# One hybrid encoder layer: which stages run beside which, and a 512-wide out-projection

## The chip, the cores and the metric

The kernel runs on one core of a Trainium2 chip. The core has five engines with instruction queues of their own: TensorE (PE in the profile; its weight loads are listed as PEld), VectorE (DVE), ScalarE (ACT), GpSimd (POOL) and SyncE (SP), which here issues every DMA. SBUF is the working memory, PSUM holds matmul results in eight banks, DRAM holds inputs, outputs and scratch tensors. The metric is device microseconds (us) of one execution.

## The reference

One layer, for a prompt of 1024 tokens and for 8 decode streams of 16 new tokens each, which share the weights. The kernel packs both into 9 tiles of 128 tokens (8 of the prompt, one of all samples). All is float32; D_MODEL 1024, 16 heads of 64, half of them in group A and half in B.

```python
h = rmsnorm(x, g_mix)
q_a, k_a, v_a, q_b, k_b, v_b = split_heads(h, w_in)      # w_in: 1024 x 3072
# group A, causal, full past: stick-breaking
z = q_a @ k_a * 64 ** -0.5
w = exp(log_sigmoid(z) + sum of log_sigmoid(-z) over the keys behind, strictly causal)
a = w @ v_a
# group B, own chunk of 64 and the 8 chunks before: softmax with a relative bias
o_b = softmax(q_b @ k_b * 64 ** -0.5 + bias) @ v_b
x = x + concat(rmsnorm(a, g_out_sb), rmsnorm(o_b, g_out_cb)) @ w_out
h = rmsnorm(x, g_ffn)
x = x + (silu(h @ w_gate) * (h @ w_up)) @ w_down         # width 2816
x = x + sigmoid(rmsnorm(x, g_ple) @ w_ple_gate) * (p @ w_ple_proj)
y = rmsnorm(x, g_final)
```

The prompt attends to itself. Each decode stream attends to its cache (A: 1024 past keys, B: 512) and its own 16 tokens. The new keys and values are outputs too.

## The kernel before

**Arithmetic.** Every matrix product is three matmuls (`mm3`, L103 to L106) of a high and a low part of each operand: high x high, high x low, low x high. So each operand is split: ScalarE copies the high part, GpSimd (weights, V caches) or VectorE (what comes out of PSUM) subtracts it for the low part (`Chunks.parts`, L148 and L109).

**Stages.** The source lists them in this order, some as generators that yield after each step, so that `advance(main, side, ratio)` can take steps of two in turn:

1. Norm of the 9 token tiles and their transposes into `hT` (L187 to L197).
2. `qkv_group(0)`: A's projection, k, v, then q, 256 columns of `w_in` at a time. k and v are made token tile by token tile (24 matmuls of 256 columns, then a yield; 18 yields for two chunks); q comes out transposed, three token tiles at a time (24 matmuls of 384 columns, 12 yields). Results go to the DRAM tensors `qkT` and `vhl`, in parts.
3. `qkv_group(1)`, B's projection, beside `decode` at 0.8 decode steps per projection step. `decode` runs through A's 8 streams and then B's; a step handles 256 cached keys (512 KB, tile `draw`): a K chunk is transposed (L367), split (`dhi`, `dlo`) and multiplied with q (`sdec`); a V chunk is split and multiplied with the transposed weights (L442, L443). A stream has 4 K and 4 V chunks in A, 2 and 2 in B. `RAWS` = 2 chunks are held raw. A's weights come from a sigmoid on ScalarE (L400), the causal factor and 1 - w on GpSimd (L412, L414) and a running product on VectorE (L416).
4. `attention(range(8))`: 8 pairs of heads (4 of A, 4 of B), 128 units of one head and 128 queries, over the prompt. A unit's scores come from L555 and L556. In A two sigmoids give `w` and `keep` (L560, L561), VectorE scans `keep` (L569), GpSimd multiplies (L570); in B VectorE adds the bias `toep` and takes the maximum (L564), ScalarE takes the exponential (L573). Five units later (`LAG`) the weights are transposed (L589), split (`wth`, `wtl`) and multiplied with v (L612, L613). `finish` normalises a pair of heads and writes it to the DRAM tensor `mixp` (L631 to L654). In the first 64 steps `embed` (p @ w_ple_proj, tile `pj`, stored in `proj`) runs beside it at 0.5 and decode at 0.4, in the next 48 decode at 0.7, then what is left of decode.
5. The last 25 steps of attention beside `half_out` at 1.5: `mix` reads `mixp` back, transposes and scales it into `hU` (L816 to L825), 12 steps for the four pairs of A; then A's half of the out-projection in 4 column chunks of 256, 36 steps of 12 matmuls.
6. `mix` for B's four pairs, one step of `half_out` beside each of its 12, the rest of `half_out`, then `lower`: B's half of the out-projection with the FFN norm and its transposes.
7. FFN, per-layer embedding gate, final norm.

**What sets the order.** The source gives dependencies and a priority; the tile framework then lays out one fixed order of instructions for each engine at build time. An instruction can come ahead of its place in the source when its operands are ready. Each engine works through its own order. Tiles of one tag share `bufs` buffers, and a tile waits for the release of the buffer that it takes; pools on the left and right side of SBUF and of the PSUM banks (`banks`) are opened and closed like stacks, so a new stage's tile waits for the old tiles in its place. `ch` is the weight pool: one raw buffer (`wraw`) and two pairs of `whi`, `wlo`. The attention borrows these: `qk` and `vk` take the tags `whi` and `wlo`, `osb` in `finish` takes `wraw`.

## Time and profile before

| | |
|---|---|
| median of 3 runs | 1923.48 us (1921.3 to 1924.91) |
| profiled execution | 1920.99 us, span of the trace 1919.2 us |
| PE matmuls | busy 1833.9 us (96% of the span), 11998 instructions |
| VectorE | busy 823.2 us (43%) |
| ScalarE | busy 718.2 us (37%) |
| GpSimd | busy 722.3 us (38%) |
| DMA | 220.60 MB, mean 115 GB/s |
| granted PE clock | 0.991 of full speed |

The span is the time from the first to the last instruction on the core; the run time has about 1.8 us around it. Busy time is the union of an engine's instructions. Matmuls overlap each other in the pipeline, so that a row's duration is longer than the distance to the next one's start. In rows of groups, the columns are: line, engine, operation, tiles (out<-in), shapes, count | busy us, mean ns of one | idle time of the engine just before them, and what ended it. All steps of one kind share the line of their helper: L104 to L106 are every `mm3`, L109 every low part, L133 every load of weights and caches.

### The profile page before, as it was taken

What the parts mean: (1) busy time and instruction counts of PE and PEld (TensorE: products, weight loads), DVE (VectorE), ACT (ScalarE), POOL (GpSimd) and SP (SyncE); (2) the same over time, 40 slices, a digit from 0 to 9 for tenths busy, and PEclk for the clock granted to TensorE, in tenths of its full rate; (3) what the DMA queues carried; (4) which work ended last, traced back from release to release, by engine and by line L of the source; (5) the groups of instructions that cost most, each with busy time, mean ns of one, the idle gap of its engine ahead of it and who ended that gap; (6) DMA issues with size and microseconds to landing.
All of it is one profiled execution on the core that took longest, in us unless ns stands there. A gap on an engine that the chain in (4) does not pass through costs nothing.

```text
span 1919.2 us, 30012 instructions
## 1 busy us (share of the span) xinstructions
PE 1833.9 (96%) x11998; PEld 1733.7 (90%) x11998; DVE 823.2 (43%) x1590; ACT 718.2 (37%) x1545; POOL 722.3 (38%) x600
## 2 busy tenths in 40 slices
PE   7999999988888798899999999999999999999998
PEld 7999999987777688889999999999999999999898
DVE  5201332347888888783541331321322312313735
ACT  5322444347778687872241111111111111121532
POOL 4232345446567744523022223223223223122355
PEclk9999999999999899999999999999999999999999
DMA  6555556576558576773011111111111101111133
GB/s 214 201 176 177 183 192 203 172 229 184 161 144 218 150 223 196 214 234 117 12 45 45 44 44 44 44 45 44 45 44 44 44 29 38 44 45 44 36 98 132
DMA packets 166011, 220.60 MB, mean 115 GB/s; under 512 B 14576, under 2 KB 118768, under 8 KB 165872
## 3 DMA queue, kind: packets, MB, share of 16 engines
q1 hardware_dynamic: 165872, 218.69, 37.2%
q8 instruction: 95, 1.56, 0.4%
q14 instruction: 44, 0.36, 0.1%
HBM read 168.84 MB, written 49.81 MB: 114 GB/s over the span
## 4 chain that ended last, share of the span: by engine, by line
PE 61%; DVE 5%; DMA 3%; ACT 3%; POOL 2%; issue 1%; SPq 0%; POOLq 0%; ACTq 0%; DVEq 0%
PE ps L104 16%; PE ps L105 16%; PE ps L106 16%; PE acc L104 2%; PE acc L106 2%; DVE keep L569 2%; PE acc L105 2%; DMA draw<-in_cache_cb_v 1%; PE pt L589 1%; DVE wtl L109 1%; PE pt L613 1%; PE pt L187 1%; PE pt L612 1%; PE pt L367 1%; ACT dhi L148 1%
## 5 line engine op out<-in xcount | busy, mean ns | idle before, releaser
L109 POOL TENSOR_TENSOR wlo<-wraw,whi 128x1024 fp32r<-128x1024 f32 (+1 forms) x118 | 257.2, 2200 | 605.1 <-ACT whi L148 605.1
L106 PE MATMUL ps<-hUh,wlo 128*128 128x384 f32 x1056 | 352.9, 334 | 0.0
L104 PE MATMUL ps<-hUh,whi 128*128 128x384 f32 x1056 | 352.9, 334 | 0.0
L105 PE MATMUL ps<-hUl,whi 128*128 128x384 f32 x1056 | 352.9, 334 | 0.0
L148 ACT CAST whi<-wraw 128x1024 fp32r<-128x1024 f32 (+1 forms) x118 | 107.6, 962 | 328.0 <-PE ps L106 227.4
L923 DVE TENSOR_TENSOR x<-x,ps 128x512 f32<-128x512 f32 x198 | 135.9, 687 | 158.3 <-PE ps L106 158.3
L104 PEld LDWEIGHTS ps<-hUh,whi 128*128 128x128 f32 x1056 | 198.2, 188 | 0.4
L105 PEld LDWEIGHTS ps<-hUl,whi 128*128 128x128 f32 x1056 | 198.2, 188 | 0.4
L106 PEld LDWEIGHTS ps<-hUh,wlo 128*128 128x128 f32 x1056 | 198.2, 188 | 0.0
L104 PE MATMUL ps<-whi,hTh 128*128 128x256 f32 x576 | 165.4, 287 | 0.7 <-ACT sth L215 0.6
L105 PE MATMUL ps<-wlo,hTh 128*128 128x256 f32 x576 | 164.6, 286 | 1.0 <-POOL wlo L109 1.0
L106 PE MATMUL ps<-whi,hTl 128*128 128x256 f32 x576 | 165.0, 287 | 0.0
L109 POOL TENSOR_TENSOR dlo<-draw,dhi 128x1024 fp32r<-128x1024 f32 x48 | 117.8, 2455 | 102.1 <-ACT dhi L148 95.3
L105 PE MATMUL ps<-wlo,acth 128*128 128x512 f32 x396 | 156.2, 394 | 0.0
L104 PE MATMUL ps<-whi,acth 128*128 128x512 f32 x396 | 155.3, 392 | 0.0
L106 PE MATMUL ps<-whi,actl 128*128 128x512 f32 x396 | 153.8, 388 | 0.0
L909 DVE TENSOR_TENSOR tmp<-sg,ps 128x384 f32<-128x384 f32 x66 | 36.6, 555 | 235.4 <-PE ps L106 235.4
L907 DVE TENSOR_TENSOR sg<-tmp,ps 128x384 f32<-128x384 f32 x66 | 36.5, 554 | 197.7 <-ACT tmp L906 197.7
L109 POOL TENSOR_TENSOR actl<-tmp,acth 128x384 fp32r<-128x384 f32 x66 | 66.5, 1007 | 133.8 <-ACT acth L910 133.8
L105 PEld LDWEIGHTS ps<-wlo,hTh 128*128 128x128 f32 x576 | 111.0, 193 | 1.3 <-POOL wlo L109 1.3
L104 PEld LDWEIGHTS ps<-whi,hTh 128*128 128x128 f32 x576 | 111.0, 193 | 1.1 <-ACT sth L215 0.8
L569 DVE TENSOR_TENSOR_SCAN keep<-keep,zero 128x128 f32<-128x128 f32 (+3 forms) x64 | 105.7, 1658 | 14.1 <-ACT keep L561 11.0
(187 smaller groups left out, 4439.4 us busy)
## 6 DMA issues: line engine op xcount, KB each, us to landing
draw<-in_cache_sb_k SPq DMA_DIRECT2D x32, 512.0 KB, 4.4
draw<-in_cache_sb_v SPq DMA_DIRECT2D x32, 512.0 KB, 3.9
wraw<-in_w_in SPq DMA_DIRECT2D x12, 1024.0 KB, 5.5
wraw<-in_w_gate SPq DMA_DIRECT2D x11, 1024.0 KB, 5.4
wraw<-in_w_up SPq DMA_DIRECT2D x11, 1024.0 KB, 5.5
wraw<-in_w_down SPq DMA_DIRECT2D x11, 1024.0 KB, 4.9
v<-sv SPq DMA_DIRECT2D x12, 768.0 KB, 4.1
x<-in_x_prompt SPq DMA_DIRECT2D x16, 512.0 KB, 6.4
```

The costliest lines, as they stand in the source:

```text
L104: T.matmul(out, lhsT=ah, rhs=bh, start=start, stop=False)
L105: T.matmul(out, lhsT=ah, rhs=bl, start=False, stop=False)
L106: T.matmul(out, lhsT=al, rhs=bh, start=False, stop=stop)
L109: eng.tensor_tensor(out, a, hi.bitcast(F32), op=ALU.subtract)
L148: A.copy(h[:, o], v[:, o])
L187: T.transpose(pt[:, j * P : (j + 1) * P], h[:, c : c + P], ident)
L367: T.transpose(pt[:, pr * P : (pr + 1) * P], raw[:, m, pr * P : (pr + 1) * P], ident)
L569: V.tensor_tensor_scan(rev, rev, zero[:, 0:1].to_broadcast([P, n]), 1.0, op0=ALU.mult, op1=ALU.add)
L589: T.transpose(pt[:, (c - c0) * P : (c - c0 + 1) * P], w[:, c * P : (c + 1) * P], ident)
L907: V.tensor_tensor(out[0][:, f, s], t_, ps, op=ALU.mult)
L909: V.tensor_tensor(t_, sg[:, f, s], ps, op=ALU.mult)
L923: V.tensor_tensor(x1[t][:, o], x1[t][:, o], ps, op=ALU.add)
```

## The change

Stages are paired in another way.

- `qkv` replaces the two calls of `qkv_group`: A's q, A's k, of A's v the third token group (tiles 6 to 8, in which the samples are) of both column chunks, 36 steps that run alone; then the rest of A's v and B's k, 30 steps; then B's v and B's q, 30 steps.
- `decode` takes its group as an argument and is made twice. Decode A runs beside the 30 steps of A's v and B's k at 2.2. Decode B runs beside B's attention, followed by `embed` (`chain`), at 1.3 for 42 attention steps.
- The attention's first 58 steps run beside B's v and q (1.95 per projection step), 42 beside decode B and `embed`, the last 37 beside `half_out` at 1.0.
- In decode, `keep` is a second sigmoid on ScalarE; the causal mask is a matmul that adds -1e30; V chunks come `VLAG` items later; `RAWS` is 4.
- `qk` and `vk` have buffers of their own; `keep` in the attention has three buffers for four, `obt` one for two, `stl` one for two.
- v is split and written per token tile (36 writes of one tile for 12 of three).
- The out-projection is 512 columns wide: `half_out` has 18 steps for 36, `lower` one 512-wide half more. All its weights go through `ch`.
- Pools and banks move with the stages; `dynamic_dma_scratch_size=1024` reserves less SBUF for DMA descriptors.

```diff
-LAG, RAWS, PT = 5, 2, 2
+LAG, RAWS, PT = 5, 4, 2
+VLAG = (2, 1)
...
-            hl = [stg.tile([P, 384], F32R, name=f"st{x}", tag=f"st{x}")[:, :n] for x in "hl"]
+            hl = [stg.tile([P, 384], F32R, name=f"st{x}", tag=f"st{x}", bufs=1 + (x == "h"))[:, :n] for x in "hl"]
...
+        loads = [(0, 0, 0), (0, 0, 1), (0, 1, 0), (0, 1, 1), (0, 2, 0), (0, 2, 1),
+                 (1, 1, 0), (1, 1, 1), (1, 2, 0), (1, 2, 1), (1, 0, 0), (1, 0, 1)]
...
+        load(0, 4)
+        for i, (grp, w, c) in enumerate(loads):
+            if (grp, w, c) == (0, 2, 1):
+                continue
+            load(i + 1)
+            wts = ready[grp, w, c]
+            if w == 0:
+                yield from queries(grp, c, wts)
+            elif (grp, w) != (0, 2):
+                yield from others(grp, w, c, wts, range(3))
+            elif c == 0:
+                yield from others(0, 2, 0, wts, (2,))
+                yield from others(0, 2, 1, ready[0, 2, 1], (2, 0, 1))
+                load(i + 2)
+                yield from others(0, 2, 0, wts, (0, 1))
...
+        ks = [("k", n, c) for n in range(8) for c in range(nkc)]
+        vs = [None] * (nkc + VLAG[grp]) + [("v", n, c) for n in range(8) for c in range(nkc)]
+        seq = [x for pieces in zip_longest(ks, vs) for x in pieces if x]
...
             if grp == 0:
+                if last:
+                    T.matmul(sc[:, 256:], lhsT=identb, rhs=causalb, start=False, stop=True)
                 A.activation(w, sc, AF.Sigmoid)
+                A.activation(st["keep"][:, own], sc, AF.Sigmoid, scale=-1.0)
...
-                G.tensor_tensor(w[:, n_old:], w[:, n_old:], causal, op=ALU.mult)
-                keep = dk.tile([P, n_all], F32, name="keep", tag="keep", bufs=1)
-                G.tensor_scalar(keep, w, -1.0, 1.0, op0=ALU.mult, op1=ALU.add)
...
-            qk = qp.tile([P, 2 * D], F32R, name="qk", tag="whi", bufs=2)
-            vk = qp.tile([P, 2 * D], F32R, name="vk", tag="wlo", bufs=2)
+            qk = ap_.tile([P, 2 * D], F32R, name="qk", tag="qk", bufs=2)
+            vk = ap_.tile([P, 2 * D], F32R, name="vk", tag="vk", bufs=2)
...
-                keep = ap_.tile([P, (5 + t % 4) * P], F32, name="keep", tag=f"keep{t % 4}")[:, :n]
+                keep = ap_.tile([P, (7, 8, 6)[t % 3] * P], F32, name="keep", tag=f"keep{t % 3}")[:, :n]
...
-    for _ in qkv_group(0, ch, hT, stg, ps["o"], ps["t"]):
-        pass
+    project = qkv(ch, hT, stg)
+    advance(project, None, 0, 36)
...
-    advance(qkv_group(1, ch, hT, stg, ps["o"], ps["t"]), dec, 0.8)
-
-    left.close()
+    banks(dstack, "right", d=2, a=1)
+    dp = pool(first, "dA", "left")
+    dec = decode(0, Chunks(dp, "d", 1088, RAWS, 2, 1024), dp)
+    advance(project, dec, 2.2, 30)
+    for _ in dec:
+        pass
+    first.close()
+    dstack.close()
+
     banks(left, "left", s=2, t=3)
+    banks(right, "right", o=3)
     at = pool(left, "at", "left")
     att = attention(ch.pool, at, ps, LAG)(range(8))
+    advance(project, att, 1.95)
+    right.close()
+
+    banks(dstack, "right", d=2, a=1)
+    dp = pool(dstack, "dB", "right")
+    dec = decode(1, Chunks(dp, "d", 1088, RAWS, 2, 1024), dp)
...
-    pj = embed()
-    advance(both(att, pj, 4, 0.5), dec, 0.4, 4 * 2 * NP)
-    for _ in pj:
-        pass
-    pstack.close()
-    advance(att, dec, 0.7, 48)
-    for _ in dec:
+    beside = chain(dec, embed())
+    advance(att, beside, 1.3, 42)
+    for _ in beside:
         pass
...
-        for c in range(4):
-            wh, wl = wp.load(w_out[0, :512, c * 256 : (c + 1) * 256].rearrange("(k p) c -> p k c", p=P), 4, 256)
+        for c in range(2):
+            wh, wl = out_weights(0, c)
...
-                acc = ps["m"].tile([P, 256], F32, name="acc", tag="M")
+                acc = ps["m"].tile([P, 512], F32, name="acc", tag="M")
...
-    advance(att, side, 1.5, N4)
-    w_b = [upper(ch, 0, 512)]
-    advance(att, side, 1.5)
+    advance(att, side, 1.0)
     left.close()
```

More of the change, by code (lines that the diff above doesn't have):

```diff
@@ new lines, in queries @@
+        def queries(grp, c, wts):
+            wh, wl = wts
+            for pr in range(2):
+                m = slice(pr * P, (pr + 1) * P)
+                for g in range(3):
+                    ps_ = ps["o"].tile([P, 384], F32, name="ps", tag="O")
+                    for k in range(KT):
+                        mm3(ps_, wh[:, k, m], wl[:, k, m], *hT.rows(g, k), k == 0, k == KT - 1)
+                    transposed_out(grp, 0, c * 2 + pr, g, parts(384, ps_, HD**-0.5))
+                    yield
@@ L310, in decode @@
+        nc.sync.dma_start(sv.bitcast(F32).rearrange("p c h x d -> p c (h x d)"),
+                          vhl[grp][:, NP * P :, :].rearrange("c p n -> p c n"))
+        new["v"] = [sv[:, :, :, x, :] for x in range(2)]
         qbd = []
@@ L863, in tile_hymba_step @@
         pass
-    w_b += [upper(wp, c, 256) for c in (2, 3)]
+    w_b = [out_weights(1, c) for c in range(2)]
     ps_o = ctx.enter_context(tc.tile_pool(name="p3o", bufs=4, space=PSUM, reuse_waits="tile"))
@@ L871, in lower @@
         acc = ps_o.tile([P, 512], F32, name="acc", tag="O")
-        for n, w in (((512, w_b[0]),), ((256, w_b[1]), (256, w_b[2])))[half]:
-            o = slice(0, 512) if n == 512 else slice(256 * (w is w_b[2]), 256 * (w is w_b[2]) + 256)
-            for k in range(4):
-                mm3(acc[:, o], *hT.tok(t, 4 + k), w[0][:, k], w[1][:, k], k == 0, k == 3)
+        for k in range(4):
+            mm3(acc, *hT.tok(t, 4 + k), w_b[half][0][:, k], w_b[half][1][:, k], k == 0, k == 3)
         xs = x1[t][:, half * 512 : half * 512 + 512]
```

255 lines of the change are left out of this document (107 added, 148 removed).

## The prediction

> **What bounds the kernel now.** I read the page's slices first, then the sums per stage, and only then who waits for whom. Slices of 48 us:
>
> ```profile
> PE   7999999988888798899999999999999999999998
> ```
>
> TensorE (PE) falls short of 9 in the first slice and in most of slices 9 to 18; behind 975 us it is full. The sums by stage (columns: stretch, its length, then busy us and instructions of PE, weight loads, VectorE, ScalarE, GpSimd, then clock, DMA share, GB/s) put borders to that:
>
> ```profile
> 0.00:47.00 47.00, 35.38 (x257) 34.29 (x258) 24.89 (x40) 25.94 (x47) 20.20 (x29) 1.00 0.65 211
> 47.00:204.00 157.00, 156.32 (x1179) 155.62 (x1178) 23.10 (x44) 41.88 (x79) 42.08 (x30) 1.00 0.55 186
> 204.00:412.00 208.00, 208.00 (x1632) 207.73 (x1631) 71.31 (x113) 80.84 (x158) 88.07 (x81) 1.00 0.59 189
> 412.00:656.00 244.00, 201.11 (x1376) 171.91 (x1374) 201.81 (x263) 179.94 (x433) 166.93 (x129) 0.97 0.64 176
> 656.00:829.00 173.00, 155.95 (x1209) 148.14 (x1208) 140.60 (x482) 138.51 (x349) 81.27 (x108) 0.96 0.74 205
> 829.00:932.00 103.00, 98.51 (x733) 89.66 (x732) 54.66 (x144) 43.31 (x97) 30.77 (x23) 1.00 0.50 152
> ```
>
> These are: norm and first projections; A's projection; B's projection beside decode A; A's attention beside decode and embed; B's attention beside decode; A's half of the out-projection. A busy PE is not a full one, so I price its work by spacing in stretches of one kind of matmul (three rows of sums for PE alone, one of the timeline):
>
> ```profile
> 88.00:113.00 25.00, 25.00 (x211) 1.00 0.58 197
> 1077.00:1126.00 49.00, 49.00 (x285) 1.00 0.13 43
> 1052.00:1076.00 24.00, 24.00 (x106) 1.00 0.15 44
> 25.84 0.93 PE L187 MATMUL pt<-ident,hrow 128*128 128x128 f32 x7
> ```
>
> 256 wide: 25/211 = 0.119 us. 384: 0.173. 512: 24/105 = 0.229. Transposes: (0.93 - 0.28)/6 = 0.108. I count the groups by shape in each stage; for 412 to 656 they run, 32 groups, from
>
> ```profile
> L589 PE MATMUL pt<-ident,w 128*128 128x128 f32 x266 | 42.0, 282 | 12.9 <-DVE ob L620 6.6 <-POOL w L570 5.8 <-DVE wtl L109 0.4
> ...
> L383 PE MATMUL pt<-ident,wn 128*128 128x128 f32 x4 | 1.1, 287 | 1.1 <-POOL wn L430 1.1
> ```
>
> That makes 177 us of work in 244, 141 in 173, 92 in 103: PE idles **67 + 32 + 11 = 110 us** from 412 to 932, against nothing in 204 to 412, where projection matmuls fill each wait. In 412 to 656 VectorE (202 of 244) and GpSimd (167) are the crowded ones. Who PE and the queue SP wait for there (us in total, times, longest):
>
> ```profile
> PE pt L589 <- DVE ob L620: 10.0, 5, 5.1
> PE pt L367 <- DMA draw<-in_cache_cb_k: 4.3, 4, 1.8
> PE pt L367 <- DMA draw<-in_cache_sb_k: 4.1, 4, 1.6
> SPq L133 <- POOL dlo L109: 46.1, 20, 6.1
> SPq L133 <- PE pt L367: 42.1, 16, 7.1
> ```
>
> No single wait is large: work is missing there, and it was spent earlier.
>
> **The change, part by part.** Nearly all PE work stays; what moves is idle time. I list the idle time that I expect in place of the 110 us.
>
> *Out-projection.* The 256-wide matmuls of it are
>
> ```profile
> L104 PE MATMUL acc<-whi,hUh 128*128 128x256 f32 x216 | 62.1, 288 | 0.8 <-DVE x L841 0.6 <-DVE hUl L825 0.2
> ```
>
> three such lines: 648 x 0.119 = 77.1 us become 324 x 0.229 = 74.2: **-3 us**. So 113 us can be had.
>
> *Start.* q comes first and needs three normed tiles per group where k needed one. Of 47 us, 30 were work (257 matmuls). Tiles follow each other in some 3 us, so the first group comes up to 6 us later, but then has 8.3 us of work per three tiles: **+3** (0 to 8). A's k and a third of v follow, dense as in 47 to 204: +0.
>
> *Decode A beside A's v and B's k.* Decode work on PE: a K chunk has 8 transposes and 12 matmuls (2.3 us), a V chunk 2 and 8 (1.2), a batch 0.8 more: 32 x 3.5 + 6 = 118 us. The 30 projection steps: 30 x 24 x 0.119 + 4 = 90. Sum 208. Decode's own changes:
>
> ```profile
> L414 POOL TENSOR_SCALAR keep<-wdec 128x1040 f32<-128x1040 f32 x8 | 9.4, 1174 | 0.4
> L412 POOL TENSOR_TENSOR wdec<-wdec,causal 128x16 f32<-128x16 f32 x8 | 2.2, 281 | 0.8 <-ACT wdec L400 0.2
> L400 ACT ACTIVATE wdec<-sdec 128x256 f32<-128x256 f32 (+1 forms) x32 | 12.4, 387 | 33.3 <-PE sdec L106 33.3
> ```
>
> GpSimd loses 11.6 us, ScalarE gains 32 sigmoids (12.4), PE 8 tiny matmuls (under 1). Today's stage 204 to 412 has the same 30 steps and 18 of the 32 K chunks:
>
> ```profile
> 204.00:412.00 208.00, 19.12 (x144) 16.45 (x144) 17.87 (x17) 40.77 (x17) 1.00 0.59 189
> kT0l<-stl SPq DMA_DIRECT2D x12, 192.0 KB, 3.0
> ```
>
> (sums of the instructions on `draw` alone: 144 transposes, 8 a chunk; below it a row of the DMA issues with the us to landing). Even that whole stage times 32/18 is VectorE 127, ScalarE 144 + 12, GpSimd 157 - 12: none reaches 208, so PE hides them. The smaller v writes (36 for 12) and the second `stl` buffer that is gone are covered by 2.9 us of matmuls per step; uncovered, B's 12 k writes cost 12 x 3.0 = 36. DMA: 64 x 0.52 MB plus some 15 MB of writes and weights in 213 us is 227 GB/s; today's stage moved 189, but
>
> ```profile
> 840.00:860.00 20.00, 17.80 (x130) 14.81 (x129) 17.07 (x48) 16.07 (x38) 5.55 (x5) 1.00 0.95 305
> ```
>
> shows 305. At 189 the stage would take 256 us (+48). I take **+5**, near the zero of 204 to 412; bounds 0 to 48.
>
> *Attention A beside B's v and q.* 58 of A's 64 units. PE: 101 us of projection (18 x 24 x 0.119 + 12 x 24 x 0.173) and 58/64 of 109 = 99 (A's units at the same prices: 288 transposes 31, scores 34, outputs 36, masks and finishes 8; B's come to 89): 200 in all. VectorE and GpSimd:
>
> ```profile
> L569 DVE TENSOR_TENSOR_SCAN keep<-keep,zero 128x128 f32<-128x128 f32 (+3 forms) x64 | 105.7, 1658 | 14.1 <-ACT keep L561 11.0 <-POOL wlo L109 2.8
> L570 POOL TENSOR_TENSOR w<-w,keep 128x127 f32<-128x127 f32 (+3 forms) x64 | 86.3, 1354 | 66.6 <-DVE keep L569 63.7 <-PE pt L589 2.8
> L115 POOL TENSOR_TENSOR r_o<-r_o,nhalf 128x16 f32<-128x16 f32 x8 | 25.3, 3163 | 8.9 <-DVE r_o L114 8.7
> L651 POOL TENSOR_TENSOR osb<-osb,r_o 128x512 f32<-128x512 f32 x16 | 19.6, 1247 | 0.3
> ```
>
> VectorE: scans 58 x 1.66 = 96; all of today's stage, decode and embed included, times 58/63 is 186. GpSimd: 58 x 1.35 = 79, finishes 3.5 x (3.16 + 2 x 1.25) = 20, four weight loads
>
> ```profile
> L109 POOL TENSOR_TENSOR wlo<-wraw,whi 128x1024 fp32r<-128x1024 f32 (+1 forms) x118 | 257.2, 2200 | 605.1 <-ACT whi L148 605.1
> L109 POOL TENSOR_TENSOR sv<-st,sv 128x768 fp32r<-128x768 f32 x12 | 22.2, 1847 | 37.2 <-ACT sv L262 37.2
> ```
>
> 8 x 2.2 = 18, half of the v splits 11: 128. PE is the longest again. Three `keep` buffers for four: a unit's sigmoids, scan and product take about 1.5 + 1.7 + 1.4 us, and three units pass in 3 x 200/58 = 10, so hidden; if not, that is the upper bound's case. qk/vk no longer take the weight buffers; `osb` still shares the raw one. I take **+12** (6%, as this chain has more links than decode's); bounds 0, and 62 (58 units at today's 67/63 us).
>
> *Attention B beside decode B and embed.* It waits for the last q step, whose memory and banks it takes. PE: 10 (last A units) + 50 (36 units of B) + 62 (decode B) + 27 (embed) = about 150. Today's twin, 656 to 829, held 54 units and nearly all of decode B; three quarters of its attention leaves VectorE some 120 and ScalarE, with embed, some 130. It idles 23% of its work; its best stretch,
>
> ```profile
> 680.00:740.00 60.00, 57.35 (x465) 54.65 (x464) 52.68 (x191) 52.27 (x136) 29.51 (x42) 1.00 0.82 227
> ```
>
> by shapes 55 us of work in 60, about 8%. Here PE leads VectorE by more, and four raw buffers for two take most of the 8.4 us of draw waits: **+20**; bounds 7 and 35.
>
> *Attention B's rest beside A's out-projection.* 39 + 4 + 50 = 93 us of PE. At ratio 1.0 its 30 steps end some seven before the attention's 37. Then the last head has to be finished; today (VectorE and GpSimd in the timeline):
>
> ```profile
> 869.25 0.43 DVE L620 TENSOR_TENSOR ob<-pt,obt 64x256 f32<-64x256 f32 x1 [1.33 <-ACT obt L619]
> 881.16 2.04 POOL L651 TENSOR_TENSOR osb<-osb,r_o 128x512 f32<-128x512 f32 x2
> ```
>
> 14 us from the last output to the end of its scaling (883.2), then the write and the read back
>
> ```profile
> mixp<-osb SPq DMA_DIRECT2D x8, 512.0 KB, 4.9
> mixn<-mixp SPq DMA_DIRECT2D x16, 192.0 KB, 3.4
> ```
>
> 8 us together: 22 us. Today out-projection steps lie on top of it, up to 932. Now only `mix` of earlier heads (4 us) and up to 8 us of `lower` can: 10 bare, with the thin end of the attention 15, and 5 until A's `mix` has its first rows: **+20**; bounds 5 and 30.
>
> *Gate, FFN, end*: the first gate weights now wait for a pair that `lower` frees after its first halves; three `lower` and transposes behind that, some 11 us of PE work, lie over the 1.7 us that a first quarter takes to convert: +0 (2 if bare). All behind it is unchanged.
>
> **Sum.** 1919.2 - 110 - 3 + 3 + 5 + 12 + 20 + 20 = 1866 span; run time was 1920.99 for a span of 1919.2, and the median of the three runs, 1923.48, is 2.5 above that. From the profiled run's own time the sum gives 1920.99 - 53 = **1868 us** (own range 1849 to 1886); the 2.5 are less than any term, so I leave them out.
>
> **Rivals.** *Scans and GpSimd's work exclude each other.* Then attention A lasts 96 + 128 = 224 us, not 212: **1879** (and decode A's stage nothing more: 8 scans in 208). For it: a scan of 128 elements and a cast of 64 take very different times (min/median/max):
>
> ```profile
> L569 DVE TENSOR_TENSOR_SCAN keep<-keep,zero x64: 392/1696/3595, 413.8 to 660.4; 128x128 f32<-128x128 f32 x8, 128x256 f32<-128x256 f32 x8, 128x384 f32<-128x384 f32 x8, 128x512 f32<-128x512 f32 x8
> L359 POOL CAST qbd<-sq x64: 226/234/2024, 193.4 to 772.4; 64x64 fp32r<-64x64 f32 x64
> ```
>
> Against: nearly all scans (105.7) and GpSimd's 167 lie in 412 to 656, more than its 244, and stretched waiting is in these durations already. The Trainium skill, "SBUF — State Buffer", section "SBUF: two separate sides", states such an exclusive lock between GpSimd and a VectorE operation with two SBUF inputs; the cast's 2024 ns agrees, the 273 in 244 doesn't rule it out, as blocked time may be counted as busy.
>
> *Order holds the stalls.* PE runs its instructions in the order laid down at build time; where an attention matmul waits, the projection behind it waits too. Then attention A keeps 62 us of idle time: **1918**. For it: `L589 <- ob` waits up to 5.1 us. Against: 204 to 412 has the same fixed order beside decode and no idle time.
>
> *Packed.* All stages do as 204 to 412; only start, 8% in attention B and the bare tail remain: 3 + 12 + 11 = 26 for 60: **1834**.
>
> *Slower: draws block SP.* A draw that waits for its buffer holds up each write behind it on SP; `sth`/`stl` stay full, then the banks, then PE. Today that is 88.2 us in 36 waits, 2.45 each, of which 8.4 us (10%) reached PE. 96 draws x 2.45 = 235 us. At a third, 78 us instead of the 13 in my terms for the two decode stages: **1933**. It decides from 30% on. Against: the raw buffers are doubled.
>
> *The pairs don't form.* The order follows readiness, not the source alone:
>
> ```profile
> 4.08 2.42 SPq L738 DMA_DIRECT2D g_out<-in_g_out_sb x1
> ```
>
> stands behind all of A's projection in the source and ran at 4 us. If the stages slip back, nothing changes: 1921. But new memory and banks tie decode A to `first`.
>
> **Chances.** Forecast 0.47, exclusion 0.13, packed 0.15, order 0.15, draws 0.06, no pairs 0.04. Faster by over 0.2% (4 us, about what a measurement of this kernel can tell from no change): the first three and most of the fourth, 0.88; same 0.06; slower 0.06. The range 1830 to 1905 leaves out draws, no pairs and half of order, 0.18.
>
> **What would show it.** PE near full in the slices of attention A, with 110 us less idle time before the FFN and about 60 of it back: most in attention B and in a gap of some 10 us ahead of `lower`. Wrong: PE waiting for `draw` or `sth` beside decode A, or for `w L570` in attention A.

## The result and the profile after

The changed kernel takes **1994.4 us** (median of four runs, 1991.5 to 1997.9) beside 1923.6 for the kernel before on the same chip (four runs, one more than stood in the table above): a ratio of **1.037, 95% interval 1.0351 to 1.039**. It is slower by 71 us, and the forecast was 1868, so the forecast lies 126 us off, on the wrong side of no change. The profiled execution took 1995.0 us for a span of 1993.2. The kernel after by slices of 50 us (the page; PE, and the clock that it was granted, in tenths):

```profile
PE   5999999789997888879699999999999999999998
PEclk8999999899998899989799999999999999999999
```

There are more thin slices than before, and they come in groups: one at the start, one around 350 us, and nearly all from 600 to 1000. The clock falls in the same places. The sums by stage (columns as in the prediction) give each group its stage:

```profile
0.00:60.00 60.00, 38.72 (x192) 34.87 (x193) 30.04 (x46) 27.57 (x49) 20.09 (x29) 0.89 0.59 203
60.00:174.00 114.00, 113.93 (x877) 113.66 (x876) 17.12 (x34) 29.40 (x60) 26.02 (x23) 1.00 0.52 174
174.00:330.00 156.00, 156.00 (x1334) 155.56 (x1333) 71.18 (x106) 81.39 (x180) 77.33 (x80) 1.00 0.67 212
330.00:425.00 95.00, 69.18 (x453) 61.84 (x452) 43.56 (x62) 42.28 (x90) 50.16 (x35) 0.86 0.50 153
425.00:600.00 175.00, 173.94 (x1266) 164.35 (x1266) 123.30 (x160) 117.91 (x289) 105.65 (x79) 1.00 0.54 151
600.00:670.00 70.00, 52.97 (x350) 47.10 (x350) 47.99 (x77) 49.57 (x105) 37.08 (x48) 0.88 0.65 191
670.00:852.00 182.00, 153.62 (x1026) 135.34 (x1026) 112.08 (x371) 117.76 (x287) 65.13 (x81) 0.95 0.64 171
852.00:966.00 114.00, 101.46 (x569) 86.61 (x570) 63.21 (x194) 52.45 (x128) 20.38 (x16) 0.94 0.53 141
966.00:1045.00 79.00, 62.83 (x302) 51.66 (x301) 36.90 (x58) 28.33 (x49) 23.97 (x18) 0.87 0.28 80
```

At the prices of the prediction (0.119 us for a matmul of 256 columns and so on, each stage's matmuls counted by shape), the idle time of PE is:

| stretch of after | what runs | idle, forecast | idle, measured |
|---|---|---|---|
| 0 to 60 | norms, A's q | 17 + 3 | 32 |
| 60 to 425 | A's k; decode A beside A's v and B's k | 5 | 44 |
| 425 to 670 | attention A beside B's v and q | 12 | 34 |
| 670 to 852 | attention B beside decode B and embed | 20 | 50 |
| 852 to 1045 | attention B's rest, out-projection, bare end | 20 | 43 |
| sum | | 77 | 203 |

The kernel before idles 130 by the same count (18 of it in its first 50 us, 112 from 412 on). From the FFN on little differs: from the first gate matmul to the first matmul of the down-projection it is 81 us for 78, and from there to the end 867 in both. So the 71 us are idle time of PE: 112 us were to be filled, and 171 came back in their place, with 14 more at the start. This count takes everything above the dense prices as idle, gaps and matmuls that last longer alike. By the two pages PE stands without any matmul for 133 us of the span in after (1993.2 - 1859.9) and for 85 in before (1919.2 - 1833.9), so that about 48 of the 74 us by which the span grew are gaps, and the rest is matmuls that take longer than at dense spacing, for which the lower granted clock is one possible cause.

Two things stand out in the table of stages. Where a projection runs beside the decode or the attention (174 to 330, 425 to 600), PE is as full as forecast. But the projection runs out before its partner does. The kernel after, matmuls that read `hTh` alone (the projection's), by stretch (PE and weight loads, busy us and count):

```profile
174.00:330.00 156.00, 89.06 (x448) 71.20 (x448) 0.00 (x0) 0.00 (x0) 1.00 0.67 212
330.00:415.00 85.00, 1.46 (x8) 1.30 (x9) 0.00 (x0) 0.00 (x0) 0.84 0.46 149
415.00:600.00 185.00, 108.20 (x473) 78.61 (x472) 0.00 (x0) 0.00 (x0) 1.00 0.56 153
600.00:670.00 70.00, 0.00 (x0) 0.00 (x0) 0.00 (x0) 0.00 (x0) 0.88 0.65 191
```

For 85 us decode A runs almost alone (8 matmuls on `hTh`), and for 70 the end of attention A and the beginning of decode B. Who PE waits for in the first of these (us in total, times, longest):

```profile
PE po L474 <- DVE own L471: 6.1, 4, 1.9
PE acc L457 <- DVE wt L110: 5.3, 3, 3.7
PE pt L397 <- DVE dlo L110: 3.9, 3, 1.7
PE acc L458 <- POOL dlo L110: 3.6, 3, 1.3
PE sdec L105 <- ACT dhi L387: 3.5, 6, 0.7
```

These are handovers of the decode itself: PE waits for VectorE, GpSimd and ScalarE in turn, and none of its waits there is for a DMA.

### The profile page after: what moved, and what is told of

Its sections match the earlier page's. It is cut to its first block, busy times and chain, and to the rows that moved or that the text cites. A ratio compares the mean times of both kernels' runs of the same rounds, so it can differ in the third digit from the quotient of the medians.

```text
span 1993.2 us, 29599 instructions
## 1 busy us (share of the span) xinstructions
PE 1859.9 (93%) x11682; PEld 1737.9 (87%) x11682; DVE 828.1 (42%) x1573; ACT 740.4 (37%) x1595; POOL 716.5 (36%) x602
## 4 chain that ended last, share of the span: by engine, by line
PE 53%; DMA 4%; issue 3%; ACT 1%; POOL 1%; DVE 1%; SPq 0%; POOLq 0%; ACTq 0%
PE ps L105 16%; PE ps L106 15%; PE ps L107 15%; DMA proj<-pjo 1%; PE acc L105 1%; PE acc L106 1%; PE acc L107 1%; DMA mixn<-mixp 1%; PE pt L188 1%; DMA qk<-qT1l 1%; DMA vk<-kT1l 0%; PE pt L598 0%; POOL dlo L110 0%; PE pt L829 0%; DMA vk<-v 0%
## 5 line engine op out<-in xcount | busy, mean ns | idle before, releaser
L110 POOL TENSOR_TENSOR wlo<-wraw,whi 128x1024 fp32r<-128x1024 f32 (+1 forms) x112 | 263.1, 2369 | 606.6 <-ACT whi L149 597.1
L578 DVE TENSOR_TENSOR_SCAN keep<-keep,zero 128x128 f32<-128x128 f32 (+4 forms) x64 | 97.5, 1528 | 37.1 <-ACT keep L570 36.6
```

Of the source, the lines that this page charges most:

```text
L110: eng.tensor_tensor(out, a, hi.bitcast(F32), op=ALU.subtract)
L578: V.tensor_tensor_scan(rev, rev, zero[:, 0:1].to_broadcast([P, n]), 1.0, op0=ALU.mult, op1=ALU.add)
```

## The experiments

Ratios are to the kernel before, with their 95% interval; "1988.2 (1.0336, 1.0317 to 1.0355)" is a median and its ratio. All diffs are to the kernel after unless it is said.

**More buffers for decode A** (pairs3_decA).

```diff
-    dec = decode(0, Chunks(dp, "d", 1088, RAWS, 2, 1024), dp)
+    dec = decode(0, Chunks(dp, "d", 1088, RAWS, 3, 1024), dp)
```

> The changed kernel with three hi/lo pairs for decode A in place of two; all else as changed. Theory C (decode A is held to some 4 us per chunk by its own chain: a chunk can't be split before the chunk two places earlier has been multiplied, so the projection beside it runs out at 330 us and the rest of decode runs bare until 415): decode A's last finish moves from 415 us to 385 or earlier, and the time falls by 20 to 40 us, from 1994 to 1955 to 1975. Rival P (the fixed order gives the projection too many turns, whatever decode could do): last finish within 10 us of 415, time within 6 us of 1994.

1988.2 (1.0336, 1.0317 to 1.0355): 6 us faster, and decode A's last output 2 us earlier. Two hi/lo pairs by themselves are not what sets its pace.

**More decode steps a projection step** (ratio33_decA).

```diff
-    advance(project, dec, 2.2, 30)
+    advance(project, dec, 3.3, 30)
```

> The changed kernel with 3.3 decode steps per projection step in place of 2.2, two pairs. Rival P (turns): decode A advances faster than 3.9 us per chunk beside the projection, the bare stretch of 85 us shrinks by a third or more, time 1955 to 1980. Theory C (chain): decode has nothing more ready to run, so the pace stays at 3.7 to 4 us per chunk and the time within 8 us of 1994.

1994.3 (1.0368, 1.0351 to 1.0385), the decode's end unmoved. The ratio of the source isn't the ratio in the trace. The matmuls and splits on `draw` from 174 to 330 us, of after and of ratio33_decA (PE, weight loads, ScalarE, GpSimd):

```profile
174.00:330.00 156.00, 23.93 (x166) 18.82 (x167) 17.85 (x17) 40.69 (x17) 1.00 0.67 212
```

```profile
174.00:330.00 156.00, 23.43 (x161) 18.32 (x162) 17.87 (x17) 40.68 (x17) 1.00 0.67 211
```

166 transposes are 21 K chunks, 17 splits 17 V chunks, and 448 matmuls on `hTh` (above) are 28 projection steps of 16: 38 chunks for 28 steps, 1.4 where the source says 2.2; and with 3.3 written, no more.

**k ahead of q** (k_first).

```diff
-        loads = [(0, 0, 0), (0, 0, 1), (0, 1, 0), (0, 1, 1), ...
+        loads = [(0, 1, 0), (0, 1, 1), (0, 0, 0), (0, 0, 1), ...
```

> The changed kernel with A's k projected ahead of A's q. The idle time of PE up to 60 us is 32 us in the changed kernel and was 17 us up to 47 us before. If that comes from q's groups of three token tiles: about 15 us of idle time at the start again and a time 10 to 15 us shorter, 1979 to 1984. If it comes from something else at the start (the order of VectorE's norms, the weight loads): within 4 us of 1994.

1983.7 (1.0302, 1.0278 to 1.0326): 11 us. The group of waits that costs PE most at the start of after (in all, times, longest), and what is left of it here (waits of PE from 0 to 60 us, one fence for each kernel):

```profile
PE pt L188 <- DVE hTl L110: 11.3, 7, 5.5
```

```profile
PE pt L188 <- DVE hTl L110: 0.8, 1, 0.8
```

**The out-projection's steps spread over more units** (tail_06).

```diff
-    advance(att, side, 1.0)
+    advance(att, side, 0.6)
```

> The changed kernel with A's out-projection taken at 0.6 steps per attention step in place of 1.0, so that about 8 of its 18 steps lie behind the attention's last step. If the 23 us of idle time at 960 to 1000 us are the bare chain finish, write, read back, mix: it falls to 8 us or less and the time by 12 to 18 us, 1976 to 1982. If the attention's end is only shifted (the out-projection missing earlier, where PE then idles): within 5 us of 1994.

1997.4 (1.0382, 1.0367 to 1.0398). From 850 to 1050 us the idle time lies in other places and is no less. In after the two largest waits behind the attention belong to the read back of what it wrote (waits of PE, 966 to 1045):

```profile
PE pt L829 <- DMA mixn<-mixp: 10.8, 2, 8.2
PE pt L829 <- DVE hUl L833: 4.1, 2, 3.4
```

In tail_06 the longest of them is 3.1 us, but a new one of 11.0 stands beside it, for weights of the out-projection (all_mended, below, has the same one).

**B's v beside decode A too** (cover_dec).

```diff
-    advance(project, dec, 2.2, 30)
+    advance(project, dec, 1.37, 48)
...
-    advance(project, att, 1.95)
+    advance(project, att, 4.9)
```

> B's v projection (18 steps, 51 us of matmuls) moves from beside A's attention to beside A's decode; nothing else changes. Theory L (each partner chain has a length of its own, some 240 us for A's decode and 240 for A's attention, and the filler only fills): the bare end of decode A (85 us long, 43 idle) goes, decode A ends at about 415 to 430, and A's attention, with 51 us less beside it, idles some 85 us instead of 34; the run comes to 1990 to 2005. Rival N (the bare stretch itself is the loss, attention A packs whatever is beside it): decode A's 43 us of idle time go and nothing comes back, 1950 to 1960.

1996.6 (1.039, 1.0369 to 1.041): the time that theory L gives, though decode A ends later than it says (444 us) and the attention idles less (some 60 us for 85). cover_dec by stretches:

```profile
174.00:330.00 156.00, 154.39 (x1314) 153.66 (x1314) 68.28 (x101) 82.00 (x176) 78.74 (x76) 1.00 0.65 205
330.00:450.00 120.00, 109.16 (x849) 107.07 (x848) 48.25 (x74) 56.23 (x125) 74.59 (x59) 0.93 0.58 180
450.00:530.00 80.00, 78.30 (x514) 73.91 (x513) 51.60 (x68) 46.28 (x114) 29.10 (x28) 1.00 0.56 151
530.00:670.00 140.00, 109.75 (x708) 91.63 (x707) 116.93 (x161) 105.47 (x244) 86.22 (x77) 0.90 0.56 147
```

The thin 85 us at the decode are nearly filled (19 us idle in 330 to 450, at its end), and the attention is bare from 530 to 670, with 55 us idle, where it was bare from 600 to 670 with 28. The filling was moved, not added to.

**Nothing beside the two** (alone): A's v and B's k in front of the decode, B's v and q in front of the attention.

```diff
-    advance(project, dec, 2.2, 30)
+    advance(project, None, 0, 30)
...
-    advance(project, att, 1.95)
+    advance(project, None, 0)
+    advance(att, None, 0, 58)
```

> Nothing beside A's decode and beside the first 58 units of A's attention: A's v and B's k projection run in front of the decode, B's v and q in front of the attention. Theory L (lengths of their own): decode A alone still takes 220 us or more, the 58 units alone 200 us or more, TensorE about half busy in both; the run comes to about 2130. Rival S (they were slow since they shared TensorE, ScalarE and VectorE with the projection): decode A alone takes about 150 us (118 us of work), the 58 units about 130 (99 us of work), and the run comes to about 1965.

2078.2 (1.081, 1.0793 to 1.0827), between the two forecasts and nearer to theory L's; both lengths lie under its bounds of 220 and 200. The two stages of alone (sums by stretch):

```profile
250.00:454.00 204.00, 155.37 (x1067) 139.71 (x1066) 110.19 (x148) 104.31 (x222) 107.50 (x95) 0.89 0.51 165
560.00:750.00 190.00, 147.76 (x920) 123.71 (x921) 155.82 (x209) 139.51 (x329) 112.28 (x95) 0.87 0.49 125
```

Decode A alone needs 204 us for 122 us of matmuls at dense prices, attention A (scans from 557 to 755) 198 us. With nothing beside them, both leave PE idle for 80 us, and in neither is any other engine near full (VectorE 110 of 204, 156 of 190). The projections beside them bring 90 and 101 us of matmuls. In after the decode lasts 241 us (174 to 415) where 204 + 90 = 294 one behind the other: 53 of its 82 us were filled. The attention's scans take 239 us (428 to 667) for 198 + 101: 60 of 80 were filled. The dense work fills two thirds to three quarters, not nearly all. Neither chain is by itself longer than the stage that the prediction gave it (213 and 212 us): what fell short is the filling.

**The pairing of before in the new program** (unpair, unpair_kfirst).

```diff
-    advance(project, dec, 2.2, 30)
+    advance(project, dec, 1.1)
...
-    advance(project, att, 1.95)
...
-    advance(att, beside, 1.3, 42)
+    advance(att, beside, 0.46, 112)
```

> The kernel after with the pairing of before in the main: all of B's projection beside A's decode (1.1 decode steps a projection step), the attention of both groups beside B's decode and embed (0.46 a unit, over 112 units). All other edits stay (q first, four raw buffers, keep from ScalarE, 512 wide). Theory L: the 34 us of idle time at A's decode go, decode B stretches over the attention, and idle time there is about what it was before (90 to 110 of 412 to 932); the start keeps its 15: 1925 to 1945. Rival E (the small edits cost it, not the pairs): 1980 or more.

> As unpair, and A's k projected ahead of its q. k first alone gave 11 us. If the start's loss is independent of the pairs: 8 to 13 us below unpair, so 1915 to 1935 by theory L. If it only moves idle time to a later stage: as unpair, within 4 us.

2011.0 (1.0458, 1.0439 to 1.0476) and 2004.8 (1.0433, 1.0414 to 1.0451): theory L missed by over 65 us, and the time is that of rival E. unpair by stretches:

```profile
200.00:478.00 278.00, 274.60 (x2197) 273.37 (x2195) 100.29 (x171) 130.57 (x280) 140.84 (x125) 1.00 0.61 192
502.00:750.00 248.00, 200.52 (x1320) 174.85 (x1321) 199.66 (x308) 191.14 (x431) 157.51 (x143) 0.89 0.52 134
750.00:935.00 185.00, 153.53 (x923) 129.84 (x921) 120.01 (x422) 122.02 (x312) 36.51 (x40) 0.90 0.62 172
```

The first stage is dense and ends 66 us later than that of before (412), since the whole of decode A lies in it. But the attention, with that much less decode beside it, lasts as long as in before: from its first scan to its last exponential 432 us (505.8 to 937.9), in before 434 (413.8 to 847.6). It isn't the pairing of before after all: there, 14 of the 32 K chunks of decode A ride under the attention. So the run doesn't tell the pairs from the small edits. Why the attention isn't shorter without those chunks stays open; the granted clock in it is 0.89 and 0.90, in before 0.97 and 0.96. The change also gave the attention three `keep` buffers for four and one `obt` for two, and no run takes these alone. In after, ScalarE waits 5.1 us for a `keep` buffer from 428 to 600, which is too little for the whole difference, but their part isn't known.

**Decode B spread over all of B's attention** (decB_08).

```diff
-    advance(att, beside, 1.3, 42)
+    advance(att, beside, 0.8, 64)
```

> B's decode and embed go at 0.8 a unit over 64 units of B's attention, not 1.3 over 42; nothing else changes. In after, 25 units beside 33 decode steps took 133 us (663 to 796), 14 units beside 18 embed steps 56, 37 units beside the out-projection 114. Theory D (decode B's own pace holds up the units beside it): B's attention is as fast as in unpair (185 us for 64 units), the run comes to 1950 to 1970. Theory F (a unit takes some 2.9 us and a step of decode adds its own matmul time, wherever it lies; only dense matmuls fill the gaps): the steps only change their place, 1985 to 2000.

1977.9 (1.0275, 1.0258 to 1.0292), between the theories. The softmax exponentials of B's attention, one a unit (duration min/median/max, first and last start), in after and in decB_08:

```profile
L582 ACT ACTIVATE w<-w,mxp x64: 390/786/858, 684.7 to 951.1; 128x640 f32<-128x640 f32 x32, 128x128 f32<-128x128 f32 x8, 128x256 f32<-128x256 f32 x8, 128x384 f32<-128x384 f32 x8
```

```profile
L582 ACT ACTIVATE w<-w,mxp x64: 387/771/882, 674.4 to 876.5; 128x640 f32<-128x640 f32 x32, 128x128 f32<-128x128 f32 x8, 128x256 f32<-128x256 f32 x8, 128x384 f32<-128x384 f32 x8
```

The units take 202 us in place of 266, though the same decode and embed lie among them. Most of that is no gain: in after, 192 matmuls of the out-projection lie in this stretch, 44 us at dense prices, and in decB_08 none. Theory D shows better in the last step of each decode batch, here the 8 of B, in after and then in decB_08:

```profile
L484 DVE TENSOR_SCALAR ow<-on,r_d x8: 246/254/2351, 685.2 to 801.1; 128x64 f32<-128x64 f32 x8
```

```profile
L484 DVE TENSOR_SCALAR ow<-on,r_d x8: 244/255/2441, 682.9 to 807.5; 128x64 f32<-128x64 f32 x8
```

From the first of these to the last it is 116 us with 25 units of attention among them, and 125 with 36 (and 17 matmuls of embed, 4 us, fewer). Eleven units more take 9 to 13 us more, where theory F, at 2.9 us a unit, would have 32: the stretch keeps nearly the length of decode B, and that holds up the units beside it. What follows took most of the gain back. decB_08 by stretches:

```profile
660.00:874.00 214.00, 190.95 (x1355) 172.03 (x1355) 153.86 (x528) 158.28 (x397) 84.15 (x103) 0.98 0.65 186
874.00:1025.00 151.00, 125.62 (x592) 100.47 (x591) 57.86 (x101) 41.78 (x76) 32.62 (x22) 0.92 0.33 106
```

From the attention's last scores to the gate it is 151 us, in after 95 (950 to 1045), for the out-projection has only 15 units left to lie beside, and more of it comes behind them. The attention ends 75 us earlier, and the end is 56 us longer.

**More matmuls in the gaps** (double_scores_B).

```diff
+                if grp:
+                    T.matmul(sc, lhsT=hd["qq"][:, qs], rhs=hd["kkh"][:, kc], start=True, stop=True)
                 T.matmul(sc, lhsT=hd["qq"][:, qs], rhs=hd["kkh"][:, kc], start=True, stop=False)
```

> Each score matmul of B's attention with the high parts is issued twice (the first result is overwritten): 30 blocks of 128 columns a head, 8 heads, 13 to 16 us more of TensorE work beside nothing new. If the idle time there is spare (TensorE waits for others' work at the pace of VectorE and ScalarE): within 4 us of after, 1990 to 1998. If the matmuls lie on the chain from scores to weights, each one is paid: 2007 to 2012. If the lower granted clock there (0.95 for 663 to 796) comes from the gaps and is the cost: faster than after.

1994.0 (1.0373, 1.0353 to 1.0393): free. The stretch from 670 to 966 us, with all of B's scores, of after and then of double_scores_B:

```profile
670.00:966.00 296.00, 255.08 (x1595) 221.94 (x1596) 175.30 (x563) 170.21 (x414) 85.50 (x97) 0.95 0.60 159
```

```profile
670.00:966.00 296.00, 263.56 (x1700) 236.35 (x1700) 175.76 (x562) 169.68 (x415) 84.10 (x95) 0.95 0.58 158
```

PE's idle time there is spare: it waits at the pace of others, and some 100 matmuls more (8.5 us of busy time) cost nothing in it.

**One part alone in the kernel before** (before_keep, before_raws3; both with embed's `pT` single, to make room).

```diff
+                A.activation(st["keep"][:, c * 256 : c * 256 + nk], sc, AF.Sigmoid, scale=-1.0)
...
-                G.tensor_tensor(w[:, n_old:], w[:, n_old:], causal, op=ALU.mult)
-                G.tensor_scalar(keep, w, -1.0, 1.0, op0=ALU.mult, op1=ALU.add)
```

```diff
-LAG, RAWS, PT = 5, 2, 2
+LAG, RAWS, PT = 5, 3, 1
```

> The kernel before with one part of the change alone: decode A's keep as a second sigmoid on ScalarE and its mask as a matmul, in place of two GpSimd operations (11.6 us), with keep double and embed's pT single to make room. Theory L (only the pairs cost): 1915 to 1927. Rival E (the edits inside the decode slow its chain): 1935 or more.

> The kernel before with three raw buffers for decode's draws in place of two (embed's pT single to make room). The waits of TensorE for draws are 8.4 us in before. If those are on the path: 1912 to 1920. If they are covered by the next wait: within 4 us of before.

before_keep 1928.5 (1.0024, 1.0015 to 1.0034), a loss of 5 us and not a gain; **before_raws3 1915.4 (0.9956, 0.9941 to 0.9972), faster than both kernels**. What the single `pT` costs by itself no run shows. Of the change's parts, more raw buffers (three here, four in the change) are worth having by themselves. The other edits inside decode (later V chunks, new tiles), the attention's buffers and the wide out-projection weren't tried alone.

**More of the decode under the attention of before** (before_r04, before_r06; diff to before_raws3, that of r04).

```diff
-    advance(qkv_group(1, ch, hT, stg, ps["o"], ps["t"]), dec, 0.8)
+    advance(qkv_group(1, ch, hT, stg, ps["o"], ps["t"]), dec, 0.4)
...
-    advance(both(att, pj, 4, 0.5), dec, 0.4, 4 * 2 * NP)
+    advance(both(att, pj, 4, 0.5), dec, 0.7, 4 * 2 * NP)
```

> before_raws3 with more of the decode under the attention: 0.4 decode steps a projection step in place of 0.8, and 0.7 a unit in place of 0.4 for A's attention (0.7 for B's stays). Some 19 decode steps, 35 us of matmuls, move. Theory G (the attention's length, 456 us in before and 453 in unpair, is its own, and decode under it costs little): the projection stage ends 25 to 35 us earlier, the attention stays within 10 us of its 437, and the run comes to 1885 to 1900. Rival F (a step adds its matmul time wherever it lies): 1912 to 1920. Rival D (decode's own pace holds up the units beside it): 1930 or more.

> The same half way: 0.6 a projection step, 0.55 a unit of A's attention. Theory G: 1898 to 1908. Rival F: 1912 to 1920. Rival D: 1920 to 1930. If the order laid down does not follow the ratio: as before_raws3, within 4 us.

1929.2 (1.0036, 1.0022 to 1.005) and 1931.0 (1.0055, 1.004 to 1.007). Theory G falls; both lie within about 1 us of the edge of what theory D gave (1930 or more; 1920 to 1930). before_raws3, then before_r04, by stage:

```profile
204.00:412.00 208.00, 208.00 (x1632) 207.73 (x1631) 71.41 (x113) 81.04 (x158) 88.06 (x81) 1.00 0.59 189
412.00:652.00 240.00, 200.25 (x1352) 171.50 (x1350) 201.94 (x258) 178.33 (x429) 169.28 (x128) 0.96 0.61 172
652.00:834.00 182.00, 167.53 (x1319) 157.71 (x1319) 158.06 (x540) 153.36 (x389) 87.75 (x113) 0.99 0.77 214
```

```profile
204.00:377.00 173.00, 173.00 (x1327) 172.75 (x1327) 41.22 (x66) 52.74 (x104) 55.77 (x44) 1.00 0.51 167
377.00:656.00 279.00, 238.49 (x1652) 208.46 (x1650) 242.22 (x303) 207.07 (x487) 223.06 (x163) 0.94 0.64 186
656.00:850.00 194.00, 174.14 (x1343) 164.58 (x1343) 164.78 (x554) 157.29 (x398) 94.88 (x119) 0.96 0.72 204
```

The 35 us saved in the projection's stage come back as 39 in attention A's: VectorE goes from 202 to 242 busy us, GpSimd from 169 to 223. Under attention A, decode is paid for in full, and a little more.

**Room and depth for decode A** (wide_decA, ahead2_decA). wide_decA has three pairs and the transposes of the decode's weights in the projection's banks; ahead2_decA also prepares two chunks ahead.

```diff
-            pt = ps["d"].tile([P, 512], F32, name="pt", tag="T")
+            pt = ps["d" if grp else "t"].tile([P, 512], F32, name="pt", tag="T")
```

```diff
-        prepare(0)
+        ahead = 1 if grp else 2
+        for i in range(ahead):
+            prepare(i)
...
-            if i + 1 < len(seq):
-                prepare(i + 1)
+            if i + ahead < len(seq):
+                prepare(i + ahead)
```

> The kernel after with three hi/lo pairs for decode A and its weights' transposes in the projection's two PSUM banks, so that its K transposes have two banks for themselves. If banks and pairs together set decode A's pace (4 us a chunk): its last finish moves from 415 to 390 or earlier and the run to 1965 to 1980. If it is the chain of handovers inside a chunk: the last finish stays at 408 or later, the run at 1985 to 1995.

> wide_decA, and A's decode makes two chunks ready ahead of the one that it consumes, not one. If the chain inside a chunk sets the pace: the last finish of decode A moves from 405 to 375 or earlier, the bare stretch goes and the run comes to 1950 to 1965. If VectorE, ScalarE and GpSimd in their fixed order set it whatever is ready: the last finish at 400 or later, the run within 5 us of wide_decA's 1981.

1980.7 (1.0307, 1.0291 to 1.0322) and 1967.2 (1.0235, 1.0217 to 1.0253). The last step of each decode batch, 8 for A (duration min/median/max, first and last start), in after, wide_decA and ahead2_decA:

```profile
L484 DVE TENSOR_SCALAR ow<-on,r_d x8: 244/246/255, 236.6 to 415.3; 128x64 f32<-128x64 f32 x8
```

```profile
L484 DVE TENSOR_SCALAR ow<-on,r_d x8: 245/253/255, 224.3 to 407.5; 128x64 f32<-128x64 f32 x8
```

```profile
L484 DVE TENSOR_SCALAR ow<-on,r_d x8: 245/246/2357, 224.2 to 392.4; 128x64 f32<-128x64 f32 x8
```

415, 408, 392: decode A ends 23 us earlier and the run is 27 us shorter. In ahead2_decA the projection lasts until about 370 us instead of 330, so it covers more of the decode. The depth of the decode's own chain is a part of its pace. wide_decA lies between its two cases (390 and 408), and ahead2_decA, at 392, misses the 375 forecast, so the depth isn't all.

**The mendings together** (kfirst_decB08: k first and decode B at 0.8; all_mended: ahead2_decA with both).

> k first (gave 11 us) and decode B at 0.8 (gave 16) together in the kernel after. If both are independent: 1964 to 1970. If one only moves idle time into the place of the other: 1975 or more.

> ahead2_decA with k first and decode B at 0.8. If the idle time found in each place is its own: 1955 or below. If a gain ahead of the attention is eaten by the attention and what follows it, as k first was beside decode B at 0.8 (1976 in place of 1967): 1960 to 1975. In either case above the 1915 of before_raws3, if the pairing itself holds the rest.

1976.1 (1.0285, 1.0268 to 1.0302) and **1951.9 (1.0157, 1.0138 to 1.0176)**. k first, worth 11 us by itself, is worth 2 beside decB_08. Each alone brought 11 and 16 to after, both together 18 to after and 15 to ahead2_decA: in kfirst_decB08 a gain ahead of the attention is mostly eaten behind it, while all_mended comes in just under the 1955 of its first case. all_mended gives back 42 of the 71 us and stays 30 above the kernel before. Its end, from the last scores of the attention to the gate:

```profile
845.00:996.00 151.00, 125.30 (x590) 100.31 (x589) 57.66 (x100) 41.77 (x75) 32.41 (x22) 0.92 0.33 106
```

It lasts 151 us with 35 of them idle at the prices above; in before the same stretch, 846 to 975, has 129 us and 6 idle. Both kernels reach their last scores at the same time (845 and 846 us), so that what all_mended lacks lies behind them: 22 us here, and 7 from the first gate matmul to the first matmul of the down-projection (85 us for 78). The largest wait of PE in the stretch is not the attention's (waits of PE, 845 to 996):

```profile
PE acc L105 <- ACT whi L149: 12.6, 2, 11.4
```

It is for the first weights of the out-projection, from 867 to 878 us. Their load goes out only behind the write of the attention's last `osb` (SyncE):

```profile
867.57 0.42 SPq L665 DMA_DIRECT2D mixp<-osb  x1
871.26 0.39 SPq L134 DMA_DIRECT2D wraw<-in_w_out  x1
```

`osb` takes the raw buffer of the weights, and in the change all weights of the out-projection go through that buffer; before, with a weight pool of its own for A's half, loads its first ones at 588 us. The load follows the last such write by 3.7 us here, by 3.8 in decB_08 and in tail_06, and in tail_06 SyncE's wait for that write is on record (2.7 us). decB_08 has the same wait, 11.1 us, and tail_06 one of 11.0 for its second weights; after has 0.7, and there the out-projection's matmuls begin at 892 us, amid the attention. A raw buffer for `osb` alone wasn't tried, nor more units left for the end beside the other mendings.

## Why the prediction was wrong

*Out-projection, -3.* Not tested by itself. The trace has the 3 x 144 matmuls of 512 columns that the step counted on (324 new ones beside the 108 of before). That its weights now share one raw buffer with `osb` was priced at nothing; it costs 0.7 us in after, and 11 in the runs that move the out-projection behind the attention.

*Start, +3.* The mechanism was right, the size not: 15 us more idle time than before, and k first got 11 of it back. The step took it that tiles follow in 3 us; it left out what the start does besides. The waits for `hTl` are for VectorE, which had fallen behind: the longest, 5.5 us, ends just behind a normed row that took 3.37 us (last section).

*Decode A beside A's v and B's k, +5.* **This is the step that failed first, and by the most.** It summed each engine's work over the stage, found none above PE's 208 us, and took the 0 idle time of 204 to 412 as the nearest row: the projection was to fill every wait of the decode. But in that stretch of before, only 18 of 32 K chunks pass in 208 us, so the decode had more time than its chain needs. Asked for its whole work, it lasts 204 us alone, with PE idle for 82 of them. That would still fit into the 213 us of the step; the overlap does not come. The projection went through at 28 steps for 38 chunks, was over at 330 us, and filled 53 of the 82, and the decode lasts 241. The sum of busy times says nothing of that. Idle: 44.

*Attention A beside B's v and q, +12.* The same error: 198 us alone, 239 beside the projection. The stretch with the projection is nearly dense (6 us idle), the 70 behind it is not (28). Idle: 34.

*Attention B beside decode B and embed, +20.* Here two chains of handovers were laid side by side, and neither is dense. By decB_08, decode B's length held the units up; by double_scores_B, PE was free meanwhile. The step priced the stage by its best stretch in before, in which the decode was thinner (0.7 steps a unit in the source, 1.3 in after). Idle: 50, above the step's bound of 35.

*Rest and bare end, +20.* The wait for the read back is where the step saw it (8.2 us at the longest), but the sum is 43, above the bound of 30. tail_06 and decB_08 lessen this wait and have the one for the out-projection's weights in its place.

Over the five stages the idle time is 12 + 39 + 22 + 30 + 23 = 126 us above the forecast, as much as the whole miss.

*The rivals.* Draws block SP, but that doesn't reach PE: SP waits 146 us for buffers of draws from 60 to 960 us, and PE waits for a draw once, 5.0 us, at the start of decode B. Of the other signs of being wrong that the prediction named, PE never waits for `sth`, and for the weights `w` of A's attention 3.3 us in all. Exclusion: the row of scans given for it mixes eight widths (128 to 1024 columns), so its spread alone shows little; the scans take 97.5 us in after and took 105.7 in before, so they did not become longer. (Its 224 us for 212 give 1880, not 1879.) Order holds the stalls is the nearest, but not in its mechanism: beside the projection PE is nearly full, and the idle time lies where no projection is left. ratio33_decA shows that the mix of the two streams isn't the one written. Its price, 50 us, stood on the attention alone. Apart from draws (1933), no case of the prediction ends slower than before: a stage that gets worse than today's twin was not among them.

*What remains open.* The 30 us left after the mendings lie behind the attention's last scores; 11 of them are the wait for weights, read from the trace, but no run took them away. What sets the 204 and 198 us of the two chains alone was not found; the depth of the decode is a part of the first. And why the attention of unpair isn't faster than that of before: the small edits are not cleared of it.

## What to carry to other kernels

Before you lay two streams side by side, measure how long each lasts alone, not only how busy it keeps each engine: a stage is no shorter than its slower chain, and it can be a good deal longer, as dense work beside the chain fills less idle time than it lasts (here 90 us filled 53, 101 filled 60). Such work is a fixed stock: drawn together beside one chain, it leaves another bare. Look at whether the ratio written in the source is the one in the trace, and at which buffers two stages share: here weights could not be fetched before the attention gave a buffer back.

## What the runs showed of the hardware

The granted clock falls where PE is broken up: 1.00 in 174 to 330 of after, 0.84 in the bare 330 to 415. The Trainium skill, "TensorE: Matmul & The Clock Gate", section "HAM oscillation — how this bites in real kernels", says that waits between bursts of matmuls let the clock fall back; the trace agrees in direction. How much of the stage's length it makes was not measured: double_scores_B put more matmuls into the gaps and left both the clock (0.95) and the time as they were.

One normed row at the start of after took 3.37 us on VectorE where the median is 1.28, while GpSimd split a weight (timeline of GpSimd, then of VectorE: start, us, operation):

```profile
29.63 2.35 POOL L110 TENSOR_TENSOR wlo<-wraw,whi 128x1024 fp32r<-128x1024 f32 x1
```

```profile
29.69 3.37 DVE L198 SCALAR_TENSOR_TENSOR hrow<-x,r_n,row_grow 128x1024 f32<-128x1024 f32 x1 [1.26 <-POOL r_n L116]
```

GpSimd's split began 0.06 us earlier and ended at 31.98; 31.98 + 1.28 = 33.26, and the row ended at 33.06. So VectorE seems to have done nearly nothing until GpSimd was done, and its record shows the whole time as busy. This fits the exclusive lock that the prediction's first rival named; it is one row, and 2.1 us.
